# Two-block layer: the second block's feed-forwards with tokens stationary, five of eleven up groups as seven block products for eight

## The chip, the cores and the metric

The kernel runs on one core of one Trainium2 chip. The metric is the device time of one execution in microseconds (us). The figure for the kernel before is the median of 3 runs, 3347.05 us (3345.95 to 3347.32).

## The reference

Two blocks run one after the other over 256 tokens of width 2048, all in fp32. The first block (a state-space branch, a gated delta rule, a gated feed-forward with a short convolution) is not touched. The second block is

```python
h = h + 0.5 * swiglu(rmsnorm_2(h, ffn1_norm[l]), ffn1_w_in[l], ffn1_w_out[l])
u = rmsnorm_2(h, mix_norm[l]) @ w_in_mix[l]
...
h = h + jnp.concatenate([y_pool.astype(h.dtype), y_gla.astype(h.dtype)], axis=-1) @ w_out_mix[l]
h = h + 0.5 * swiglu(rmsnorm_2(h, ffn2_norm[l]), ffn2_w_in[l], ffn2_w_out[l])
```

with a final norm behind it, and

```python
def swiglu(h, w_in, w_out):
    gu = h @ w_in
    gate, up = gu[..., :D_FF], gu[..., D_FF:]
    return (jax.nn.silu(gate) * up) @ w_out
```

`D_FF` is 5632, so that each feed-forward has an up product of 256 x 2048 x 11264 and a down product of 256 x 5632 x 2048. The mix (`w_in_mix`) has four groups of trailing-window means (pool) and four heads of gated linear attention (GLA) with queries, keys, values, an output gate and a gate of low rank.

## The kernel before

**Products in three passes.** Every weight block arrives as 128 x 1024 fp32 (512 KB, `load_w`, line 78, tile `wr`, 4 buffers, on SP's queue). `split_w` (line 113) makes two fp32r tiles of it: ScalarE (ACT) copies the rounded part to `wh` (line 118), VectorE (DVE) subtracts it from the raw block into `wl` (line 119). Each has 3 buffers, and both instructions are raised in priority by 600. Activations are kept as such pairs too. A product is then hi x hi + hi x lo + lo x hi, accumulated in fp32 in a bank of PSUM.

**Four ways to multiply.** `gemm` (line 138) keeps a 128 x 128 weight block stationary and moves 256 tokens, three matmuls a block (lines 127 to 129). `gemm2` (line 153) does the same with two: the hi weights against both token halves of the pair in one matmul of 512 columns (line 162), and the lo weights in one of 256 (line 164). Its result lies in two halves of a bank, which `join` (line 217) adds. `gemm_t` (line 171) keeps 128 tokens stationary and moves 512 weight columns, three matmuls for each 128 tokens and 128 rows of weights (lines 184 to 186). `gemm_halves` (line 194) is a variant for the last quarter. `gemm`, `gemm2` and `gemm_t` use pool `pg` (4 banks); the others' banks come from `bank()` (line 63), pool `px` (4 banks).

**The feed-forward.** `ffn` (line 1024) is called for the first block and twice for the second (`f1`, `f2`; there `conv_w` is None). It cuts the 5632 hidden columns into 44 blocks of 128. `up_group` (line 1030) runs `gemm2` for gate and up of each block, joins, multiplies by the norm's factor spread over partitions, applies Silu and splits the product (`hid`): the hidden tiles come out transposed, as `gemm_t` wants them. `down_group` (line 1055) adds their product into the residual in four quarters of 512 columns by `into_x` (line 1012), which calls `gemm_t`. Group 0 has 4 blocks, groups 1 to 5 have 8; `up_group(c)` runs ahead of `down_group(c - 1)`.

**The mix.** 16 `gemm` for queries, keys and values, 8 for the pool and 8 for the gate, after one narrow product for the low-rank gate. The values are transposed back to tokens on partitions by TensorE in `gla_head` (line 1139, transposes in lines 1182 to 1187).

**What sets the order.** The program is written out in Python and each engine runs its list in order. The tile framework orders the lists by priority (program order, unless raised) and inserts all waits, also for free buffers. Work that is to lie beside products is put in by hand: `flush` (line 134) emits what is in `pend` at a fixed step of a product (`turn`, line 307: TensorE transposes of the residual and the next pairs), and `pump` (line 328) takes one step of the generators in `lanes` (GLA heads, scaling of the residual).

## Time and profile before

| | |
|---|---|
| median of 3 runs | 3347.05 us |
| the profiled execution | 3348.04 us |
| its span (first to last instruction) | 3346.2 us |
| TensorE matmul (PE) busy | 3322.8 us, 99% |
| weight load (PEld) busy | 2873.8 us, 86% |
| DVE busy | 2337.0 us, 70% |
| ACT busy | 1686.4 us, 50% |
| mean DMA rate | 180 GB/s |
| mean granted TensorE clock | 0.999 of 2.4 GHz |

The profiled execution is 1 us above the median, and 1.8 us of it lie outside the span. Matmuls are pipelined and the ends that the profile gives them are modelled: a matmul of 512 columns is listed with some 390 ns, while the next one starts sooner. So the cost of a matmul is read here from start to start, not from the listed duration, and PE's 99% says that it seldom stood still for long, not that it ran at its peak.

### The profile page before, as it was taken

What the parts mean: (1) busy time and instruction counts of PE and PEld (TensorE: products, weight loads), DVE (VectorE), ACT (ScalarE), POOL (GpSimd) and SP (SyncE); (2) the same over time, 40 slices, a digit from 0 to 9 for tenths busy, and PEclk for the clock granted to TensorE, in tenths of its full rate; (3) what the DMA queues carried; (4) which work ended last, traced back from release to release, by engine and by line L of the source; (5) the groups of instructions that cost most, each with busy time, mean ns of one, the idle gap of its engine ahead of it and who ended that gap; (6) DMA issues with size and microseconds to landing.
All of it is one profiled execution on the core that took longest, in us unless ns stands there. A gap on an engine that the chain in (4) does not pass through costs nothing.

```text
span 3346.2 us, 48440 instructions
## 1 busy us (share of the span) xinstructions
PE 3322.8 (99%) x18598; PEld 2873.8 (86%) x18598; DVE 2337.0 (70%) x3718; ACT 1686.4 (50%) x2604; POOL 4.0 (0%) x22
## 2 busy tenths in 40 slices
PE   9999999999999999999999999999999999999998
PEld 8888988888888888888888888889998888888887
DVE  8999987666777767767665656656676666566565
ACT  4566656445554545446444444445464544444444
POOL 0000000000000000000000000000000000000000
PEclk9999999999999999999999999999999999999999
DMA  6555544366666666665666666665546666666665
GB/s 219 155 156 177 176 128 132 111 221 185 185 191 191 187 189 187 188 189 182 189 189 189 187 190 187 187 191 185 151 151 195 185 192 185 189 188 188 189 187 172
DMA packets 169176, 603.42 MB, mean 180 GB/s; under 512 B 18912, under 2 KB 23520, under 8 KB 168432
## 3 DMA queue, kind: packets, MB, share of 16 engines
q1 hardware_dynamic: 168368, 599.29, 58.6%
q8 instruction: 145, 2.38, 0.3%
q10 hardware_dynamic: 576, 1.05, 0.1%
q14 instruction: 87, 0.71, 0.1%
HBM read 598.16 MB, written 2.10 MB: 179 GB/s over the span
## 4 chain that ended last, share of the span: by engine, by line
PE 94%; DVE 5%; issue 1%; ACT 0%; DMA 0%; DVEq 0%; ACTq 0%
PE pt L162 29%; PE pt L164 15%; PE ptt L186 12%; PE ptt L185 12%; PE ptt L184 12%; PE pt L127 3%; PE pt L129 3%; PE pt L128 3%; DVE wl L119 1%; PE pt L228 1%; PE side L857 1%; PE side L868 1%; PE side L603 1%; PE side L638 1%; DVE t L345 0%
## 5 line engine op out<-in xcount | busy, mean ns | idle before, releaser
L119 DVE TENSOR_TENSOR wl<-wr,wh 128x1024 fp32r<-128x1024 f32 x1097 | 1342.4, 1224 | 896.3 <-ACT wh L118 895.0
L118 ACT CAST wh<-wr 128x1024 fp32r<-128x1024 f32 x1097 | 1152.4, 1051 | 1491.0 <-issue 621.6
L162 PE MATMUL pt<-h,wh 128*128 128x512 f32 x4224 | 1487.2, 397 | 0.0
L164 PE MATMUL pt<-h,wl 128*128 128x256 f32 x4224 | 1184.6, 281 | 0.0
L162 PEld LDWEIGHTS pt<-h,wh 128*128 128x128 f32 x4224 | 792.8, 188 | 192.0 <-DVE h L303 0.2
L164 PEld LDWEIGHTS pt<-h,wl 128*128 128x128 f32 x4224 | 798.0, 189 | 1.0
L186 PE MATMUL ptt<-wh,hid 128*128 128x512 f32 x1040 | 408.9, 393 | 0.0
L185 PE MATMUL ptt<-wl,hid 128*128 128x512 f32 x1040 | 407.7, 392 | 0.0
L184 PE MATMUL ptt<-wh,hid 128*128 128x512 f32 x1040 | 405.2, 390 | 0.0
L127 PE MATMUL pt<-h,wl 128*128 128x256 f32 x1024 | 296.1, 289 | 1.0 <-DVE wl L119 1.0
L128 PE MATMUL pt<-h,wh 128*128 128x256 f32 x1024 | 290.4, 284 | 0.0
L129 PE MATMUL pt<-h,wh 128*128 128x256 f32 x1024 | 290.1, 283 | 0.0
L185 PEld LDWEIGHTS ptt<-wl,hid 128*128 128x128 f32 x1040 | 195.3, 188 | 43.6
L184 PEld LDWEIGHTS ptt<-wh,hid 128*128 128x128 f32 x1040 | 195.2, 188 | 43.4
L186 PEld LDWEIGHTS ptt<-wh,hid 128*128 128x128 f32 x1040 | 195.4, 188 | 40.0
L127 PEld LDWEIGHTS pt<-h,wl 128*128 128x128 f32 x1024 | 196.4, 192 | 5.7 <-issue 2.7
L129 PEld LDWEIGHTS pt<-h,wh 128*128 128x128 f32 x1024 | 196.4, 192 | 1.2 <-issue 1.1
L128 PEld LDWEIGHTS pt<-h,wh 128*128 128x128 f32 x1024 | 196.4, 192 | 0.8
L184 PE MATMUL ptt<-wh,h 128*128 128x512 f32 x256 | 103.4, 404 | 0.0
L186 PE MATMUL ptt<-wh,h 128*128 128x512 f32 x256 | 100.2, 392 | 0.0
L185 PE MATMUL ptt<-wl,h 128*128 128x512 f32 x256 | 99.9, 390 | 0.0
L214 ACT ACTIVATE lowh<-pt 128x256 f32<-128x256 f32 x264 | 99.2, 376 | 0.0
(375 smaller groups left out, 3191.2 us busy)
## 6 DMA issues: line engine op xcount, KB each, us to landing
wr<-in_f_up SPq DMA_DIRECT2D x528, 512.0 KB, 3.6
wr<-in_f_down SPq DMA_DIRECT2D x265, 512.0 KB, 3.5
wr<-in_w_qkv SPq DMA_DIRECT2D x48, 512.0 KB, 3.6
wr<-in_w_gs SPq DMA_DIRECT2D x32, 512.0 KB, 3.6
wr<-in_w_gd SPq DMA_DIRECT2D x32, 512.0 KB, 3.6
wr<-in_w_glu SPq DMA_DIRECT2D x32, 512.0 KB, 3.6
wr<-in_w_out SPq DMA_DIRECT2D x32, 512.0 KB, 3.5
wr<-in_w_gla SPq DMA_DIRECT2D x32, 512.0 KB, 3.5
```

What stands on the lines that cost most here:

```text
L118: act.copy(out=hi, in_=raw)
L119: dve.tensor_tensor(out=lo, in0=raw, in1=hi.bitcast(F32), op=ALU.subtract)
L127: pe.matmul(ps, wl, xt[:, 0, :], start=first, stop=False)
L128: pe.matmul(ps, wh, xt[:, 1, :], start=False, stop=False)
L129: pe.matmul(ps, wh, xt[:, 0, :], start=False, stop=last)
L162: pe.matmul(ps.rearrange("p a b -> p (a b)"), hi[:, j, :], xts[k].rearrange("p a b -> p (a b)"), start=k == 0, stop=False, skip_group_chec ...
L164: pe.matmul(ps[:, 0, :], lo[:, j, :], xts[k][:, 0, :], start=False, stop=k == n - 1, skip_group_check=True)
L184: pe.matmul(pss[t], xh, hi[:, j, :], start=k == 0, stop=False)
L185: pe.matmul(pss[t], xh, lo[:, j, :], start=False, stop=False)
L186: pe.matmul(pss[t], xl, hi[:, j, :], start=False, stop=k == n - 1)
L214: act.activation(t, ps[:, 1, :], AF.Copy, scale=scale)
L228: pe.matmul(ps, r3[:, j, :], xs[k], start=k == 0, stop=k == len(xs) - 1)
```

## The change

In the second block's two feed-forwards the up product is turned round: tokens are stationary and 512 weight columns move, as the down product had it. The 5632 hidden columns are eleven groups of 512; groups 0, 1, 2, 6, 8 and 10 are ordinary (`plain`: gate and up by `gemm_t`, 192 matmuls of 512 columns), groups 3, 4, 5, 7 and 9 go through `seven`. That halves the tokens (128 and 128), the 2048 inputs (1024 and 1024) and the columns (gate and up), and forms seven block products where the ordinary way has eight (the Winograd form of Strassen's algorithm): 28 steps of 6 matmuls. For it four sums of the activations are made once (`x_sums`) and four sums of weight blocks in every group; every block or sum that is multiplied is split into its pair. The weight block `b22` is loaded twice. Results come out with tokens on partitions, so that the hidden tiles are transposed by TensorE (`turn_hidden`, 8 transposes a group). `together` takes steps of an ordinary sequence (down products and plain groups, 12 matmuls a step) and of a sequence of sevens in turn; the four `px` banks belong to `seven` meanwhile, and `bank()` gives `pg` banks.

```diff
     def bank():
+        if side_full[0]:
+            return pg.tile([P, 512], F32, tag="pt", name="side2")
         return px.tile([P, 512], F32, tag="side", name="side")
...
+    def gemm_tg(pss, srcs, xts):
...
                 k += 1
                 if k == n // 2:
                     flush()
                 if slices[0]:
                     pump(slices[0] / 4)
-        return pss
+            yield
...
+            def turn_hidden(a, ys):
+                for i in range(2):
+                    pb = v3(bank(), T)
+                    for j in range(2):
+                        for t in range(2):
+                            f = P * (2 * i + j)
+                            pe.transpose(pb[:, j, P * t : P * t + P], a[t][:, f : f + P], ident)
+                    y = ys[i]
+                    act.copy(out=y[:, :, 0, :], in_=pb)
+                    sub(y[:, :, 1, :], pb, y[:, :, 0, :].bitcast(F32))
...
+            def plain(g):
+                a = [hd.tile([P, 512], F32, tag=f"a{t}", bufs=2, name=f"fa{t}") for t in range(2)]
+                pss = []
+                yield from gemm_tg(pss, [A[up][16 * g + i] for i in range(8)], hs)
+                if g == 0:
+                    late[0] = late[0]()
+                rc = late[0]
+                for t in range(2):
+                    act.activation(a[t], pss[t], AF.Silu, scale=rc[:, t : t + 1])
+                pss = []
+                yield from gemm_tg(pss, [A[up][16 * g + 8 + i] for i in range(8)], hs)
+                for t in range(2):
+                    stt(a[t], pss[t], rc[:, t : t + 1], a[t], ALU.mult, ALU.mult)
+                new_ys(g)
+                pend.append(lambda: turn_hidden(a, ys[g]))
+                pump(1)
...
+            def x_sums():
+                for j in range(8):
+                    f = hd.tile([P, 2, T], F32, tag="g", bufs=1, name="xf")
+                    s = hd.tile([P, 4, P], F32, tag="w", bufs=1, name="xs")
+                    for i in range(2):
+                        add(f[:, i, :], hs[j + 8 * i][:, 0, :].bitcast(F32), hs[j + 8 * i][:, 1, :].bitcast(F32))
+                    add(s[:, 0, :], f[:, 0, P:], f[:, 1, P:])
+                    sub(s[:, 1, :], s[:, 0, :], f[:, 0, :P])
+                    sub(s[:, 2, :], f[:, 0, :P], f[:, 0, P:])
+                    sub(s[:, 3, :], f[:, 1, :P], s[:, 1, :])
+                    e = []
+                    for i in range(2):
+                        t = hp.tile([P, 2, 2, P], F32R, tag=f"h{j + 8 * i}", name=f"sx{j}_{i}")
+                        act.copy(out=t[:, 0], in_=s[:, 2 * i : 2 * i + 2, :])
+                        sub(t[:, 1], s[:, 2 * i : 2 * i + 2, :], t[:, 0].bitcast(F32))
...
+            def seven(g):
+                ps = [px.tile([P, 512], F32, tag="side", name="side7") for _ in range(4)]
...
+                for jj in range(4):
+                    b11, b12, b22 = block(jj, 0), block(jj, 1, "ws"), block(4 + jj, 1, "ws")
+                    t1, t3 = (hd.tile([P, 1024], F32, tag="tt", bufs=2, name="tt") for _ in range(2))
+                    t2 = hd.tile([P, 1024], F32, tag=f"t2_{jj}", bufs=1, name="t2")
+                    w1 = split_raw(b11)
+                    with tc.high_priority(offset=600):
+                        sub(t1, b12, b11)
+                        sub(t2, b22, t1)
+                        sub(t3, b22, b12)
+                    passes(ps[0], lambda i: hx(2 * jj + i, 0), w1, **fl)
+                    yield
+                    passes(ps[1], lambda i: sx[2 * jj + i][0], split_raw(t1), **fl)
+                    yield
+                    passes(ps[2], lambda i: sx[2 * jj + i][1], split_raw(t2), **fl)
+                    yield
+                    passes(ps[3], lambda i: sx[2 * jj + i][2], split_raw(t3), **fl)
+                    yield
+                for jj in range(4):
+                    b21, b22 = block(4 + jj, 0), block(4 + jj, 1, "ws")
+                    t4 = hd.tile([P, 1024], F32, tag="tt", bufs=2, name="tt")
+                    with tc.high_priority(offset=600):
+                        sub(t4, b21, t2s[jj])
...
+                act.activation(a[0], ps[0], AF.Silu, scale=rc[:, 0:1])
+                add(a[1], ps[3], gs)
+                add(gs, ps[1], gs)
+                act.activation(a[1], a[1], AF.Silu, scale=rc[:, 1:2])
+                stt(a[0], gs, rc[:, 0:1], a[0], ALU.mult, ALU.mult)
+                stt(a[1], w5, rc[:, 1:2], a[1], ALU.mult, ALU.mult)
+                yield
+                yield
+                new_ys(g)
+                turn_hidden(a, ys[g])
+                yield
...
+                together([first_plain, plain(1), down_g(0), plain(2), down_g(1)], [x_sums(), seven(3), seven(4)])
+                for c in range(2, 5):
+                    together([down_g(c), plain(2 * c + 2)], [seven(2 * c + 1)])
+                if before_last:
+                    before_last()
+                for _ in down_g(5):
+                    pass
+                return
```

The second half of `seven` has three steps for each `jj`, with `b21`, `b22` and `t4`; between the halves three additions of 512 columns bring partial sums together. The first 8 steps of `plain(0)` run alone. `down_g` is `down_group` as a generator, which reads the hidden tiles of two groups.

The norm's factor is now used per token (`rstd_cols`), so that `spread` and its small TensorE product leave the feed-forwards. In the mix, `gemm` gives way to `gemm2` with `join` for queries, keys, pool and gate (24 products), the values come from `gemm_t` (192 matmuls) with tokens on partitions, and the 16 transposes of the values and their copies go. The low-rank product moves behind the first half of the values. The last gain is loaded in four quarters ahead of the last down product and not before the feed-forward. `layout` gives the weights in the new order on the host.

## Rows read from the trace of the kernel before

**Rows 1.** The page: span, and busy time of each engine.

```profile
span 3346.2 us, 48440 instructions
PE 3322.8 (99%) x18598; PEld 2873.8 (86%) x18598; DVE 2337.0 (70%) x3718; ACT 1686.4 (50%) x2604; POOL 4.0 (0%) x22
```

**Rows 2.** The chain that ended last within 1640 to 2260 us, by line.

```profile
by line: PE pt L162 42.8%; PE pt L164 21.7%; PE ptt L186 11.9%; PE ptt L185 11.8%; PE ptt L184 11.7%; PE side L314 0.1%
```

**Rows 3.** Windows: f1, f2, an up pair, a down pair, the mix.

```profile
core 0: us, PE busy (x) PEld busy (x) DVE busy (x) ACT busy (x) POOL busy (x), PEclk, DMA share, GB/s
1542.92:2284.11 741.19, 741.19 (x3908) 633.06 (x3907) 465.87 (x626) 345.26 (x482) 0.00 (x0) 1.00 0.61 187
2598.96:3340.00 741.04, 738.47 (x3883) 630.47 (x3881) 462.07 (x613) 341.70 (x472) 0.00 (x0) 1.00 0.61 186
1699.93:1790.37 90.44, 90.44 (x514) 78.47 (x513) 56.89 (x78) 42.48 (x62) 0.00 (x0) 1.00 0.61 187
1790.37:1834.31 43.94, 43.94 (x194) 36.06 (x193) 24.97 (x27) 17.44 (x18) 0.00 (x0) 1.00 0.63 192
...
2284.10:2508.20 224.10, 223.77 (x1792) 217.70 (x1790) 161.31 (x256) 117.49 (x183) 3.28 (x13) 1.00 0.53 163
```

**Rows 4.** PE's timeline, first and last of 36 steps of `gemm_t`, 25 of `gemm`.

```profile
1794.71 0.39 PE L185 MATMUL ptt<-wl,hid 128*128 128x512 f32 x1
...
1802.95 0.39 PE L185 MATMUL ptt<-wl,hid 128*128 128x512 f32 x1
...
2439.78 0.28 PE L128 MATMUL pt<-h,wh 128*128 128x256 f32 x1
...
2442.78 0.28 PE L129 MATMUL pt<-h,wh 128*128 128x256 f32 x1
```

**Rows 5.** Timeline: eight transposes between two matmuls of `gemm_t`.

```profile
2265.64 0.39 PE L186 MATMUL ptt<-wh,hid 128*128 128x512 f32 x1
...
2265.88 1.04 PE L314 MATMUL side<-ident,xt 128*128 128x128 f32 x8
...
2266.67 0.47 PE L184 MATMUL ptt<-wh,hid 128*128 128x512 f32 x1
...
2266.98 0.39 PE L185 MATMUL ptt<-wl,hid 128*128 128x512 f32 x1
```

**Rows 6.** Groups of instructions by line and shape: count, busy us, mean ns, idle before.

```profile
L119 DVE TENSOR_TENSOR wl<-wr,wh 128x1024 fp32r<-128x1024 f32 x1097 | 1342.4, 1224 | 896.3 <-ACT wh L118 895.0
L118 ACT CAST wh<-wr 128x1024 fp32r<-128x1024 f32 x1097 | 1152.4, 1051 | 1491.0 <-issue 621.6 <-PE ptt L186 549.3 <-PE pt L162 167.7
...
L360 DVE SCALAR_TENSOR_TENSOR xt<-ptt,xt 128x512 f32<-128x512 f32 x96 | 61.6, 683 | 0.8 <-PE ptt L209 0.8
...
L124 DVE TENSOR_TENSOR hid<-fa,hid 128x256 fp32r<-128x256 f32 x132 | 55.3, 419 | 0.0
...
L360 DVE SCALAR_TENSOR_TENSOR wt<-wt,pw,tm 128x128 f32<-128x128 f32 x64 | 20.4, 346 | 2.5 <-ACT tm L610 2.2
...
L864 ACT COPY dsc<-side 128x512 f32<-128x512 f32 x20 | 11.7, 586 | 35.6 <-PE side L863 35.6
```

**Rows 7.** Windows of the first block, where DVE is the busiest.

```profile
80.00:120.00 40.00, 35.38 (x248) 32.66 (x246) 38.61 (x122) 19.61 (x43) 0.00 (x0) 0.98 0.52 162
...
280.00:320.00 40.00, 40.00 (x201) 32.26 (x201) 37.51 (x70) 25.85 (x49) 0.00 (x0) 1.00 0.59 184
```

**Rows 8.** PE's timeline within the second window, 34 steps of `gemm_t`.

```profile
299.72 0.39 PE L185 MATMUL ptt<-wl,h 128*128 128x512 f32 x1
...
307.47 0.39 PE L186 MATMUL ptt<-wh,h 128*128 128x512 f32 x1
```

**Rows 9.** PE's timeline behind the mix: side products among products of `into_x`.

```profile
2508.97 0.40 PE L184 MATMUL ptt<-wh,yp 128*128 128x512 f32 x1
2509.21 1.05 PE L1218 MATMUL side<-sqg,mean_g 128*128 128x256 f32 x4
2509.91 0.58 PE L185 MATMUL ptt<-wl,yp 128*128 128x512 f32 x1
```

**Rows 10.** A wait of PE in the first block, and the clock behind it.

```profile
117.95 0.89 PE L638 MATMUL side<-xa,cmat 128*32 128x256 f32 x2 [3.58 <-DVE xa L345]
...
118.00:124.00 6.00, 6.00 (x31) 4.96 (x32) 4.98 (x13) 2.98 (x8) 0.00 (x0) 0.72 0.56 153
```

**Rows 11.** DMA: loads of up weights to landing; the window with the highest rate.

```profile
wr<-in_f_up SPq DMA_DIRECT2D x528, 512.0 KB, 3.6
...
2280.00:2300.00 20.00, 20.00 (x151) 17.71 (x150) 12.28 (x24) 9.26 (x16) 1.55 (x7) 1.00 0.69 247
```

More of the change, by code (lines that the diff above doesn't have):

```diff
@@ L1 @@
+import itertools
 import math
@@ L1012, in into_x, with into_xg @@
     def into_x(src, n, xts, scale=1.0, fin=None, gain=None, hs=None, halves=False):
+        for _ in into_xg(src, n, xts, scale, fin, gain, hs, halves):
+            pass
+    def into_xg(src, n, xts, scale=1.0, fin=None, gain=None, hs=None, halves=False):
         for q in range(4):
-            g = gemm_halves if halves and q == 3 else gemm_t
-            for t, ps in enumerate(g([src(q, i) for i in range(n)], xts)):
+            pss = []
+            srcs = [src(q, i) for i in range(n)]
+            if halves and q == 3:
+                pss = gemm_halves(srcs, xts)
+            else:
+                yield from gemm_tg(pss, srcs, xts)
+            for t, ps in enumerate(pss):
                 quarter_done(q, t, ps, scale, fin)
@@ new lines, in down_g @@
+            def down_g(c):
+                drain()
+                gs = (2 * c - 1, 2 * c) if c else (0,)
+                tiles = [y[:, j] for g in gs for y in ys[g] for j in range(2)]
+                o = 16 * c - 8 if c else 0
+                n = len(tiles) // 2
+                last = {"fin": fin, "gain": gain, "hs": nxt, "halves": gain is None} if c == 5 else {}
+                yield from into_xg(lambda q, i: A[down][o + n * q + i], n, tiles, scale, **last)
+            sx = []
+            def x_sums():
[13 more added lines that the diff above has]
+                        sub(t[:, 1], s[:, 2 * i : 2 * i + 2, :], t[:, 0].bitcast(F32))
+                        e += [(t[:, 0, c, :], t[:, 1, c, :]) for c in range(2)]
+                    sx.append(e)
+                    yield
@@ L1030, in up_group, with together @@
+            def together(seq, sevens):
+                side_full[0] = True
+                a, b = (itertools.chain(*s) for s in (seq, sevens))
+                for x, y in itertools.zip_longest(a, b):
+                    pass
+                side_full[0] = False
             def up_group(c):
@@ L1059, in down_group @@
                 into_x(lambda q, i: A[down][o + n * q + i], n, tiles, scale, **last)
+            if conv_w is None:
+                first_plain = plain(0)
+                for _ in range(8):
+                    next(first_plain)
+                together([first_plain, plain(1), down_g(0), plain(2), down_g(1)], [x_sums(), seven(3), seven(4)])
[4 more added lines that the diff above has]
+                for _ in down_g(5):
+                    pass
+                return
             prev = up_group(0)
@@ L1086, in late1 @@
         c1 = rstd_cols(n1)
-        b = spread(rstd_cols(n2, pre=c1))
+        c2 = rstd_cols(n2, pre=c1)
         def scale_x():
@@ L1095, in late1 @@
         side.append(scale_x())
-        return b
+        return c2
     h3 = [None] * KT
@@ L1181, in gla_head @@
             act.activation(ktt[:, c, :], pb[:, P * t : P * t + P], AF.Copy, scale=half[:, c % 2 : c % 2 + 1])
-        pv = v3(bank(), T)
-        for t in range(2):
-            for f in range(2):
-                pe.transpose(pv[:, t, P * f : P * f + P], vts[f][:, P * t : P * t + P], ident)
-        vt = scratch(4, [P, 2, T], "vtg")
-        act.copy(out=vt, in_=pv)
         yield
@@ L1198, in gla_head @@
             pk = bank()
-            pe.matmul(pk[:, :T], ktt[:, c, :], vt[:, c // 2, :], start=True, stop=True)
+            pe.matmul(pk[:, :T], ktt[:, c, :], vt[c // 2], start=True, stop=True)
             if c == 0:
@@ L1224, in gla_head @@
         yield
+    gv = []
+    vs = values(0)
+    rm = spread(rc[0])
+    low_rank()
     slices[0] = 1
-    gv = []
     for hd in range(4):
@@ L1231, in tile_kernel @@
         hv = [gp_.tile([P, T], F32, name=f"gv{hd}_{f}") for f in range(2)]
-        for j, t in enumerate((hq, hk, *hv)):
-            ps = gemm(wsrc("w_gla", 4 * hd + j), hs)
-            if j == 0:
-                stt(t, ps, P ** -0.5, rm, ALU.mult, ALU.mult)
-            else:
-                mul(t, ps, rm)
+        if hd == 2:
+            vs = values(1)
+        joined(hq, gemm2(wsrc("w_gla", 2 * hd), hs), P ** -0.5)
+        joined(hk, gemm2(wsrc("w_gla", 2 * hd + 1), hs))
         gv += hv
-        side.append(gla_head(hd, hq, hk, hv))
+        o = 2 * P * (hd % 2)
+        side.append(gla_head(hd, hq, hk, [v[:, o : o + 2 * P] for v in vs], hv))
     def pool_group(g, up):
@@ L1286, in tile_kernel, with load_gb2 @@
     hs = h4
-    gb2 = gains(ctx, 1)
+    gb2 = []
+    def load_gb2():
+        for q in range(4):
+            gb2.append(scratch(q, [P, 512], "gb2"))
+            sp.dma_start(out=gb2[q], in_=A["gain"][1, :, q])
     def fin3(q, t, x):
```

130 lines of the change are left out of this document (96 added, 34 removed).

## The prediction, made before the changed kernel ran

> **What bounds the kernel now.** I read the page's busy times first. TensorE has 99% of the span, DVE 70%, ACT 50% [rows 1]. A busy share is an average over stages, so I went on to the chain of waits inside the first of the two feed-forwards that change: every link but 0.1% is a matmul, of `gemm2` (lines 162, 164) or of `gemm_t` (184 to 186), and no DVE, ACT or DMA stands in it [rows 2]. The windows say the same of both feed-forwards: PE busy 741.19 of 741.19 us and 738.47 of 741.04, DVE 466 and 462, ACT 345 and 342 [rows 3]. So a matmul less is time won here, one for one, for as long as DVE keeps up; and DVE is what the change loads.
>
> **The price of a matmul, start to start.** An up pair of groups (256 blocks of 128 x 128 by `gemm2`) takes 90.44 us [rows 3], 0.3533 us a block. `gemm_t` makes 36 steps in 8.24 us, 0.2289 us a matmul of 512 columns, and `gemm` 25 steps in 3.00 us, 0.1200 us a matmul of 256 [rows 4]. A down pair, 192 matmuls, takes 43.94 us [rows 3], again 0.229 each, with its changes of bank inside.
>
> The Trainium skill, page "TensorE: Matmul & The Clock Gate", section "Wait — 56ns, not 53.3ns?", gives the columns over 2.4 GHz plus 2.5 ns from start to start. By that rule a block of `gemm2` would cost an estimated 0.325 us and a matmul of 512 columns 0.216, turning the product round would win nearly nothing, and the sum below would end at 3322 us. The rows have some 15 ns a matmul on top, and I take the rows.
>
> **Up products.** Removed in each feed-forward: 88 `gemm2` of 16 blocks, 1408 x 0.3533 = 497.4 us. Added: 6 plain groups of 192 matmuls and 5 sevens of 28 x 6 = 168, together 1992 x 0.2289 = 456.0 us. That is 41.4 us each, **-82.8** for both; 28.0 of it comes from turning the product round (2112 x 0.2289 = 483.4 a feed-forward) and 54.9 from the eighth product (5 x 24 matmuls, twice). Taking turns between a plain product and a seven changes the bank oftener; the down pair's price says that this costs nothing.
>
> **Transposes.** Hidden tiles must now be turned, 8 transposes a group. Eight between two matmuls push the second next start from 0.46 to 1.34 us behind [rows 5], 0.88 us. 22 groups: **+19.4**.
>
> **The mix.** Out: 32 `gemm` x 48 x 0.1200 = 184.3 us. In: 24 `gemm2` x 16 x 0.3533 = 135.7 and 192 x 0.2289 = 43.9, together 179.6. 16 transposes of values go, at 0.11 us each 1.8. **-6.5**. The added `join` puts 24 more sums of 256 columns on DVE (0.42 us each [rows 6]), which has 161 of 224 us busy there [rows 3]: nothing. Side steps have fewer products to lie under, and one or two more fall to the end; but side products are fitted in among those of `into_x` there [rows 9]: nothing, or 4 us if not.
>
> The low-rank product, `spread` and the last gain only move; their loads are a few of 0.5 MB or less on SP's queue, and the work beside them covers them. Where `rstd_cols` now makes the first gate wait, the up half has the other two banks and 22 us of matmuls.
>
> Without any new wait this sums to -69.9.
>
> **What could uncover.** DVE first. In the stretch where sevens run, each feed-forward has 640.6 us of PE: 3048 matmuls and 11 turns are 707.4, less 22.0 (the first gate, alone) and 44.8 (the last down, alone). DVE has there 300 splits and 80 weight sums like them at 1.224 us, 465 us; the activation sums, 8 x (4 x 0.419 + 4 x 0.346) = 24.5; and 109 operations of 512 columns at 0.683 for results, additions and hidden tiles, 74.4 [rows 6]. 564 of 640.6, **88%**. In the first half of a seven it is 90%: 11 x 1.224 + 2 x 0.683 = 14.8 of 72 x 0.2289 = 16.5 us. The nearest rows: at 37.5 of 40 us, 94%, PE went 34 steps of `gemm_t` at 0.228 us, undisturbed; at 38.6 of 40, 97%, PE stood still for 4.6 us [rows 7, 8]. 88 to 90% lies on the good side, closer to the first. ACT has 324 casts of 1.051 us in 707, about half.
>
> Locally four waits are possible; each has zero as its lower bound, since there is no work they take away.
>
> - *The three weight sums* of a step stand ahead of the next split on DVE. In the worst order the cast waits for a buffer until the down step's matmuls end; cast, subtraction, three sums and the next subtraction then take 1.05 + 5 x 1.224 = 7.2 us, while PE has 1.37 + 2.75 + 1.37 + 0.23 = 5.7 us of work. 1.5 us late, 40 times: 60 us at most. The sums only need loads that come long before (3.6 us to land [rows 11]) and the framework orders by what is ready, so I take 6.
> - *The activation sums* in 8 steps of 22.0 us together: 24.5 + 8 x 1.224 = 34.3 of DVE, 12.3 over, 24.6 for both at most. Only the last sums are late, and they are wanted some 48 us later; I take 4.
> - *The turn* of a plain group stands right ahead of the down matmuls that read it. ACT copy 0.586 and DVE subtraction 0.683, behind a cast and a subtraction in flight, are 3.55 us at worst against 2.3 us of other work: 1.3 late, 6 times (groups 2, 6 and 8), and 2.7 where nothing lies beside it, twice (group 10): 13 at most. PE's list is filled by what is ready [rows 9]; I take 3.
> - *The end of the fourth group's seven* has no ordinary steps left beside it: two additions, Silu, two products, some 3.8 us, twice, 7.6 at most. The next down can begin with the third group's tiles; I take 1.
>
> **The other queues.** A seven loads 20 blocks for 16, all on SP, whose list waits for free raw buffers. First half: 7 loads of 0.524 MB in 16.5 us, 223 GB/s; 247 was reached [rows 11]. Nothing. The extra `ws` loads stand ahead of plain loads on SP, but wait only for the sums of the step before.
>
> **Sum.** -82.8 + 19.4 - 6.5 + 14 = -55.9 against the profiled execution's 3348.0 us. That lies 1.0 above the median of the runs, so I say **3291**.
>
> **Rivals.**
> 1. *Everything is covered.* The framework fits all waits in, as in the 94% stretch [rows 7, 8]. 3347.05 - 69.9 = 3277. Against it: four places at once. 0.22.
> 2. *DVE becomes the bound: slower.* DVE goes through its list in order and stood 895 us behind ACT's casts before, casts that themselves wait for PE to free a buffer [rows 6]. That was free while DVE had 37% to spare. If the same chain (matmul, buffer, cast, subtraction) keeps it from more than 82% busy in the mixed stretch, this lasts 564 / 0.82 = 688 instead of 640.6 us, 47 more a feed-forward: 3277 + 94 = 3371. It decides from 83.5% downward (564 / 0.835 = 675, 35 us more). For it: cast and subtraction are coupled by three buffers only. Against it: the 94%. 0.10.
> 3. *The clock falls in the waits.* After PE had stood 3.58 us for DVE, the granted clock of the next 6 us was 0.72 [rows 10], so part of it ran at 1.2 instead of 2.4 GHz; 6 x 0.28 = 1.7 us lost on top of the wait. If every unit of a plain group with a seven had one such wait (5 a feed-forward), that is 10 x 5.3 = 53 us: 3330. The Trainium skill, same page, section "A second HAM failure mode: psum-queue depth-cycling", has a kernel whose short pauses at each change of banks let the clock swing; this kernel changes banks far oftener than before. No row of the two feed-forwards shows it: their clock is 1.00 [rows 3]. 0.05.
> 4. *The change does less than it says.* The local waits come to half their bounds together, 53 us of 105: 3277 + 53 = 3330. 0.11.
>
> The forecast itself, 3284 to 3315, has 0.52. The range reaches from rival 1, a little lower for what the mix may give, to over rivals 3 and 4: **3272 to 3342**; rival 2 and the worst of 4 are left out. A measurement of this kernel tells 0.2%, 6.7 us, from no change. Faster: 0.52 + 0.22 + 0.05 and most of 4, less a margin for costs that I don't see, **0.84**; same **0.05**, the upper edge of 4; slower **0.11**.
>
> **What would show it.** In the changed profile: matmuls of 512 columns at 0.229 us also where sevens and plain products take turns; 240 fewer of them in the two feed-forwards than ordinary products would have; each feed-forward some 710 to 717 us long, DVE busy about 599 of it (564, and 24 splits and 8 products outside the mixed stretch), 84%; PE's list of waits with only short entries on `wl`, the transposes and the activation sums; the mix 6 us shorter; clock 1.00. Wrong would be: DVE above 94% busy for long, or below 84% with PE waiting for `wl`; a feed-forward above 735 us; a chain of waits in which DVE has more than a tenth.

## The result and the profile after

The changed kernel takes **3308.7 us** (median of 4 runs, 3307.0 to 3309.9), the kernel before 3347.2 in the same comparison: ratio 0.9883, 95% interval 0.9866 to 0.9900, 38.5 us less. Forecast were 3291, that is 56 us less. The sign and the range held; the gain is two thirds of the one forecast. The profiled execution took 3307.0 us.

The page of the changed kernel: span, busy times and the chain that ended last by engine; behind them two rows of its DMA list (KB each, median us from issue to landing) [rows 1, 11]. The last row is the chain by engine in the kernel before.

```profile
span 3305.2 us, 44334 instructions
PE 3263.8 (99%) x16530; PEld 2742.3 (83%) x16530; DVE 2568.6 (78%) x3748; ACT 1777.3 (54%) x2523; POOL 4.0 (0%) x22
PE 84%; DVE 10%; DMA 3%; issue 2%; ACT 1%; DVEq 0%; SPq 0%; ACTq 0%
...
wr<-in_f_up SPq DMA_DIRECT2D x448, 512.0 KB, 3.8
ws<-in_f_up SPq DMA_DIRECT2D x120, 512.0 KB, 4.5
...
PE 94%; DVE 5%; issue 1%; ACT 0%; DMA 0%; DVEq 0%; ACTq 0%
```

PE is still listed as 99% busy, but DVE's share of the chain over the whole kernel has risen from 5 to 10%, and that of loads from 0 to 3%. In the first feed-forward (f1) before, no DVE and no DMA stood in the chain [rows 2]; in the changed kernel DVE's splits and weight sums have 13% of it there and loads of `wr` 7% (1560 to 2220 us).

The same three stretches in the changed kernel, by windows: first feed-forward, mix, second feed-forward with the kernel's end.

```profile
core 0: us, PE busy (x) PEld busy (x) DVE busy (x) ACT busy (x) POOL busy (x), PEclk, DMA share, GB/s
1542.70:2265.40 722.70, 713.96 (x3167) 583.20 (x3167) 579.40 (x631) 388.48 (x430) 0.00 (x0) 1.00 0.62 207
2265.40:2572.35 306.95, 306.90 (x1612) 259.25 (x1611) 222.27 (x345) 167.90 (x269) 3.27 (x13) 1.00 0.52 175
2572.35:3305.20 732.85, 714.17 (x3147) 582.36 (x3145) 577.80 (x621) 385.39 (x421) 0.00 (x0) 0.99 0.61 204
```

Windows cut in the same way before have 741.20, 315.06 and 747.24 us. So f1 gives 18.5 us, the mix 8.1 and f2 14.4, together 41.0, the whole difference of the spans. In f1 PE was busy in every microsecond before [rows 3]; now it stands still for 8.7 of 722.7, and more in f2. This understates it, since a matmul behind a pause is listed longer. Counted from start to start (what lies beyond 0.2288 us for a matmul of 512 columns, beyond 0.11 for a transpose, each by more than 0.05), the losses are 17.3 us in f1 and 19.9 in f2, against less than 2 us in either before: **37 us**, where 14 were forecast. The question of the experiments is where they come from.

PE's list of waits in the changed kernel, from 1540 us to the end (us in total, times, longest):

```profile
PE side L1131 <- DVE wl L126: 9.3, 11, 1.8
PE ptt L202 <- DVE hid L367: 3.3, 4, 1.2
PE side L1130 <- ACT wh L125: 2.3, 2, 1.1
PE ptt L201 <- DVE wl L126: 1.7, 4, 0.6
PE side L1061 <- DVE fa L376: 0.9, 2, 0.6
PE ptt L200 <- ACT wh L125: 0.5, 2, 0.3
```

The largest is a seven's matmul (lines 1130 to 1132) that waits for the low part of its weights, DVE's subtraction of line 126. Two fifths of all losses sit in one place in each feed-forward: the end of group 4's seven, whose last steps have no ordinary block beside them. The windows there:

```profile
1816.00:1820.00 4.00, 4.00 (x19) 3.31 (x18) 4.00 (x6) 2.34 (x3) 0.00 (x0) 1.00 0.35 127
1820.00:1824.00 4.00, 3.24 (x14) 2.10 (x13) 3.89 (x4) 3.38 (x4) 0.00 (x0) 1.00 0.62 190
1824.00:1828.00 4.00, 1.58 (x6) 0.74 (x4) 4.00 (x4) 1.04 (x1) 0.00 (x0) 1.00 0.80 245
1828.00:1832.00 4.00, 3.51 (x12) 2.50 (x13) 2.99 (x6) 1.81 (x3) 0.00 (x0) 0.57 0.94 333
```

and what DVE and PE do in them, by the timeline (start us, us, instruction, what ended the idle time before):

```profile
1821.04 2.55 DVE L126 TENSOR_TENSOR wl<-wr,wh 128x1024 fp32r<-128x1024 f32 x2
1823.52 1.22 DVE L367 TENSOR_TENSOR t<-ws,tt 128x1024 f32<-128x1024 f32 x1
1824.65 1.22 DVE L367 TENSOR_TENSOR tt<-ws 128x1024 f32<-128x1024 f32 x1
1825.79 1.22 DVE L126 TENSOR_TENSOR wl<-wr,wh 128x1024 fp32r<-128x1024 f32 x1
1826.92 1.22 DVE L126 TENSOR_TENSOR wl<-tt,wh 128x1024 fp32r<-128x1024 f32 x1
...
1826.21 0.50 PE L1130 MATMUL side<-wh,sx 128*128 128x512 f32 x1 [1.13 <-ACT wh L125]
1828.19 0.80 PE L1131 MATMUL side<-wl,sx 128*128 128x512 f32 x1 [1.48 <-DVE wl L126]
1828.78 0.63 PE L1132 MATMUL side<-wh,sx 128*128 128x512 f32 x1
1829.21 0.63 PE L1130 MATMUL side<-wh,sx 128*128 128x512 f32 x1
...
1828.06 0.68 DVE L364 TENSOR_TENSOR fa<-side,gs 128x512 f32<-128x512 f32 x1
1830.99 1.26 PE L1061 MATMUL side<-ident,fa 128*128 128x128 f32 x7 [0.30 <-DVE fa L376]
```

Group 4's last product ends at 1822.4 us. What ought to follow on DVE are its results, then PE turns them and the next down step begins. Instead the framework has put the start of the next seven (group 5) there: on DVE its splits and two of its three weight sums (`t` and `tt`, 1823.52 to 1825.79), on PE its first two products, the second of which is the one that waits in the rows above. DVE is busy for 11.9 of 12 us (1816 to 1828), group 4's results come behind all this, from 1828.06, the turn at 1831.0, and the next ordinary block at 1832.1. Behind the waits the granted clock is 0.57 on average over the window, and matmuls start 0.43 us apart instead of 0.229, as at the lower of its two levels, 1.2 GHz. By the count from start to start this place loses 6.3 us in f1 and 9.3 in f2.

Elsewhere DVE itself stands still; its two largest waits from 1560 to 2220 us:

```profile
DVE wl L126 <- ACT wh L125: 87.0, 85, 1.7
DVE tt L367 <- DMA wr<-in_f_up: 24.6, 22, 2.5
```

The second is new: a weight sum at the head of DVE's list, whose block (`b11` or `b21`, a `wr` tile) has not landed.

### The profile page after: what moved, and what is told of

It reads as the page before. It is cut to its first block, busy times and chain, and to the rows that moved or that the text cites. A ratio compares the mean times of both kernels' runs of the same rounds, so it can differ in the third digit from the quotient of the medians.

```text
span 3305.2 us, 44334 instructions
## 1 busy us (share of the span) xinstructions
PE 3263.8 (99%) x16530; PEld 2742.3 (83%) x16530; DVE 2568.6 (78%) x3748; ACT 1777.3 (54%) x2523; POOL 4.0 (0%) x22
## 4 chain that ended last, share of the span: by engine, by line
PE 84%; DVE 10%; DMA 3%; issue 2%; ACT 1%; DVEq 0%; SPq 0%; ACTq 0%
PE ptt L202 15%; PE ptt L201 15%; PE ptt L200 15%; PE pt L169 13%; PE pt L171 6%; DVE wl L126 4%; PE side L1131 3%; PE side L1132 3%; PE side L1130 3%; DMA wr<-in_f_up 3%; PE pt L134 1%; PE pt L136 1%; PE pt L135 1%; PE pt L244 1%; DVE tt L367 1%
## 5 line engine op out<-in xcount | busy, mean ns | idle before, releaser
L169 PE MATMUL pt<-h,wh 128*128 128x512 f32 x1792 | 633.0, 398 | 0.0
L171 PE MATMUL pt<-h,wl 128*128 128x256 f32 x1792 | 502.6, 281 | 0.0
L200 PE MATMUL ptt<-wh,h 128*128 128x512 f32 x1088 | 427.6, 393 | 0.0
L201 PE MATMUL ptt<-wl,h 128*128 128x512 f32 x1088 | 423.9, 390 | 0.6 <-DVE wl L126 0.6
L202 PE MATMUL ptt<-wh,h 128*128 128x512 f32 x1088 | 424.1, 390 | 0.0
L169 PEld LDWEIGHTS pt<-h,wh 128*128 128x128 f32 x1792 | 336.4, 188 | 81.8 <-issue 1.0
L171 PEld LDWEIGHTS pt<-h,wl 128*128 128x128 f32 x1792 | 338.3, 189 | 0.6
L200 PEld LDWEIGHTS ptt<-wh,h 128*128 128x128 f32 x1088 | 204.3, 188 | 43.5 <-ACT wh L125 1.2
L201 PEld LDWEIGHTS ptt<-wl,h 128*128 128x128 f32 x1088 | 204.3, 188 | 43.4 <-DVE wl L126 1.7
L202 PEld LDWEIGHTS ptt<-wh,h 128*128 128x128 f32 x1088 | 204.3, 188 | 43.1 <-issue 0.4
L126 DVE TENSOR_TENSOR wl<-tt,wh 128x1024 fp32r<-128x1024 f32 x120 | 146.7, 1223 | 78.0 <-ACT wh L125 77.5
L134 PE MATMUL pt<-h,wl 128*128 128x256 f32 x512 | 149.3, 292 | 0.4 <-DVE wl L126 0.4
L136 PE MATMUL pt<-h,wh 128*128 128x256 f32 x512 | 145.4, 284 | 0.0
```

Source lines behind the costliest of these rows:

```text
L126: dve.tensor_tensor(out=lo, in0=raw, in1=hi.bitcast(F32), op=ALU.subtract)
L134: pe.matmul(ps, wl, xt[:, 0, :], start=first, stop=False)
L136: pe.matmul(ps, wh, xt[:, 0, :], start=False, stop=last)
L169: pe.matmul(ps.rearrange("p a b -> p (a b)"), hi[:, j, :], xts[k].rearrange("p a b -> p (a b)"), start=k == 0, stop=False, skip_group_chec ...
L171: pe.matmul(ps[:, 0, :], lo[:, j, :], xts[k][:, 0, :], start=False, stop=k == n - 1, skip_group_check=True)
L200: pe.matmul(pss[t], xh, hi[:, j, :], start=k == 0, stop=False)
```

## The experiments

All times are medians; the kernel before was run beside each set (3347.3 to 3348.1 us), and ratios are to it. Differences are against the changed kernel's 3308.7 (0.9866 to 0.9900) unless said otherwise. Edits are to the changed kernel.

### What turning the product round is worth without the sevens

```diff
-    together([first_plain, plain(1), down_g(0), plain(2), down_g(1)], [x_sums(), seven(3), seven(4)])
...
+    for step in (plain(0), plain(1), down_g(0), plain(2), plain(3), down_g(1), ..., plain(9), down_g(4), plain(10)):
+        for _ in step:
+            pass
```

> All eleven up groups plain, none as seven products; the rest of the change stays. It parts the change into what the turned product and the mix bring and what the eighth product brings. If the terms of the sum are right and only sevens bring new waits: turning -28.0, transposes +19.4, mix -8.0 from 3347.2, that is 3331, each feed-forward some 737 us, and PE hardly ever behind DVE. Then sevens have brought 3331 - 3308.7 = 22 us net of 54.9. If instead turning the product round brings waits of its own (the rival): 3340 or more.

Measured: 3326.3 us (3325.6 to 3326.9), ratio 0.9933 (0.9919 to 0.9948). Windows of f1 and f2, and the only wait in PE's list there:

```profile
1542.40:2275.55 733.15, 732.88 (x3284) 606.09 (x3283) 392.06 (x401) 317.52 (x349) 0.00 (x0) 1.00 0.57 189
2582.63:3323.80 741.17, 732.07 (x3267) 604.63 (x3265) 391.00 (x397) 315.28 (x341) 0.00 (x0) 1.00 0.57 189
PE ptt L200 <- ACT wh L125: 0.5, 2, 0.3
```

Turning and mix bring 21.8 us, 5 to 7 more than had been worked out from the rows of before, and PE hardly waits. f1's 3168 matmuls take (733.15 - 120 x 0.11) / 3168 = 0.2273 us each, not 0.2289. The sevens then bring 3326.3 - 3308.7 = 17.6 us net of the 54.9 that their missing products are worth: **37 us are given back, all of it in the sevens' stretch**.

### The activation sums ahead, so that no steps are left alone

```diff
+    early = x_sums()
     for _ in range(8):
         next(first_plain)
+        next(early)
-    together([first_plain, ...], [x_sums(), seven(3), seven(4)])
+    together([first_plain, ...], [seven(3), seven(4)])
```

> The eight steps of activation sums are taken beside the first eight steps of the first plain group, so that the two sequences of the first mixed stretch are 64 and 62 steps long and no step of a seven stands alone. Theory 'end of the stretch' (six of 70 steps alone, where DVE needs more than PE; 6.2 and 8.7 us lost there): 3308.7 - 15 = 3294, and no loss above 2 us at that place. Rival 'DVE is the bound as a whole': the loss moves elsewhere, 3303 or more.

Measured: 3322.2 us (3317.7 to 3324.1), ratio 0.9923 (0.9907 to 0.9940): slower, a miss. Its two feed-forwards say why. In f2, where nothing else happened, the loss from start to start fell from 19.9 to 13.3 us, and the one at group 4's end is gone. In f1 it grew from 17.3 to 33.1. PE's waits from 1560 to 1640 us, and ACT's timeline:

```profile
PE ptt L200 <- ACT fa L1080: 6.8, 1, 6.8
PE ptt L201 <- DVE wl L126: 2.5, 2, 1.9
...
1611.71 0.71 ACT L1116 CAST sx<-xs 128x256 fp32r<-128x256 f32 x2
1612.43 1.28 ACT L1080 ACT_TABLE_LOAD   x1
1616.81 1.26 ACT L1080 ACTIVATE fa<-ptt,rc 128x512 f32<-128x512 f32 x2 [3.09 <-DVE rc L361]
```

Only f1 has `late1`, whose norm factors (`rc`) DVE works out, and which then scales the residual, while group 0 runs. With the activation sums in the same list, `rc` came at 1616.8, and group 0's Silu held its banks until then. The end of group 4 can be mended, but not at that price.

### The weight sums without their priority

```diff
-    with tc.high_priority(offset=600):
-        sub(t1, b12, b11)
...
+    sub(t1, b12, b11)
...
```

> The weight sums are no longer raised by 600 in priority, the splits still are. Theory 'DVE stands at the head of its list for loads of sums' (25 and 26 us of DVE behind DMA): these waits shrink, the splits come earlier, 3308.7 - 5 to - 13, that is 3296 to 3304. Rival 'sums must be early since the splits of sums need them': the splits come later, 3312 or more. If DVE's total load is what counts, 3307 to 3310.

Measured: 3305.8 us (3302.5 to 3307.6), ratio 0.9871 (0.9856 to 0.9886). The interval overlaps that of the changed kernel: the priority neither costs nor brings what can be told. DVE's standing for loads stays, 25.6 us in f1.

### The weight sums on GpSimd

```diff
+            def wsub(o, a, b):
+                pool_e.tensor_tensor(out=o, in0=a, in1=b, op=ALU.subtract)
...
-        sub(t1, b12, b11)
+        wsub(t1, b12, b11)
...
```

> The weight sums (80 a feed-forward) go from DVE to GpSimd, which stands idle. DVE loses 98 us a feed-forward and all waits for loads of sums. Theory 'DVE's load': the waits of PE for wl nearly vanish except at the end of the first stretch, 3285 to 3295, if one sum takes GpSimd no more than some 5 us (there are 16 in a seven of about 120 us). Rival 'GpSimd is slow or slows DVE' (DVE's subtraction of 1.22 us gets longer, or splits wait for sums): slower than 3308.7.

Measured: 3388.8 us (3378.2 to 3392.7), ratio 1.0115 (1.0096 to 1.0134). Two rows of its groups by form:

```profile
L126 DVE TENSOR_TENSOR wl<-wr,wh 128x1024 fp32r<-128x1024 f32 x1017 | 1409.3, 1389 | 469.2 <-ACT wh L125 452.8
L1104 POOL TENSOR_TENSOR tt<-ws,wr 128x1024 f32<-128x1024 f32 x40 | 116.2, 2905 | 2192.9 <-DMA wr<-in_f_up 1926.4
```

A sum takes GpSimd 2.9 us in the row shown and 2.8 to 3.2 by its operands. DVE's subtraction grew from 1.22 to 1.39 us on average over the whole kernel (1.54 from f1 on, where the sums are), so that more came back than the 195 us that DVE was to be rid of (DVE busy 2619 us against 2569). The Trainium skill, page "SBUF — State Buffer", section "Who interferes with whom", says that a DVE instruction with two SBUF inputs contends with a GpSimd instruction that reads SBUF; these two rows agree.

### One list of steps

```diff
-    together([first_plain, plain(1), down_g(0), plain(2), down_g(1)], [x_sums(), seven(3), seven(4)])
-    for c in range(2, 5):
-        together([down_g(c), plain(2 * c + 2)], [seven(2 * c + 1)])
+    together([first_plain, plain(1), down_g(0), plain(2), down_g(1), plain(6), down_g(2),
+              plain(8), down_g(3), plain(10), down_g(4)],
+             [x_sums(), seven(3), seven(4), seven(5), seven(7), seven(9)])
```

> The mixed stretch is written as one list of steps with no stop between its parts: plain group 6 stands before the down step of groups 3 and 4, plain 8 and 10 likewise before theirs, so that the six steps that were left alone at the end of group 4 have ordinary blocks beside them, and only three steps (without block products) stand alone at the very end. If those six steps, each with 1.37 us of matmuls against 1.22 us of VectorE, are the place where about 15 us of the 36 us of waits arise (6.3 in the first feed-forward, 9.4 in the second), the time falls from 3308.7 to about 3294, and the excess between matmuls near 1820:1832 and 2850:2870 is gone. If VectorE is short over the whole stretch and the loss only moves to the steps after, the time stays above 3303.

Measured: 3307.3 us (3300.2 to 3309.9), ratio 0.9877 (0.9862 to 0.9891): no difference, and the profiled run is the fastest of the four. The window of group 4's end, and PE's waits at the new end, 2195 to 2225 us:

```profile
1816.00:1836.00 20.00, 20.00 (x90) 16.55 (x89) 14.65 (x15) 11.68 (x12) 0.00 (x0) 1.00 0.65 210
PE side L1061 <- DVE fa L376: 4.7, 1, 4.7
```

The old loss is gone entirely, and a new one of 6.6 us in each feed-forward has come at the end of group 9, whose results are now worked out, turned and read with nothing beside them. So the place is where it was said to be, but the time is not won: a seven's end without cover has moved. (Of the six steps that the expectation counts only three are products; the others are the results and the turn.)

The same list without the priority:

> The same list of steps, and the weight sums without their priority (they stand in the order in which they are written). The order alone gave 3305.83 against 3308.7. If the two losses are apart, about 3291; if the priority only matters where nothing stands beside the seven's steps, the same as the one list of steps alone, within 3 us.

Measured: 3311.5 us (3311.0 to 3312.5), ratio 0.9893 (0.9878 to 0.9908). With two losses apart it should have been the faster one. The gain of 3 us above was no gain.

### No weight sums at all

This kernel leaves the sums out and so does not compute the layer.

```diff
-    raw = hd.tile([P, 1024], F32, tag=tag, bufs=2, name="ws")
+    raw = hd.tile([P, 1024], F32, tag=tag, bufs=4, name="ws")
...
-    t1, t3 = (hd.tile([P, 1024], F32, tag="tt", bufs=2, name="tt") for _ in range(2))
...
+    t1, t2, t3 = b12, b22, b22
...
+    t4 = b21
```

> Leaves out the sums of weight blocks: the seven products take the blocks as they are loaded, so matmuls, loads and splits keep their number, and 16 subtractions of 1.22 us per seven (195 us of VectorE in all) are gone; the raw blocks get four buffers in place of two. If the waits come from the sums (VectorE's time, and its standing still for the sums' loads), nearly all of the 36 us go: about 3275 to 3280. If they come from the activation sums, the turning and the start of each group, the time stays above 3295.

Measured: 3282.3 us (3279.9 to 3284.2), ratio 0.9803 (0.9787 to 0.9819), **26.4 us less**. From start to start it loses 7.8 + 7.3 us, of which 5.4 and 4.2 are at group 4's end. Windows before, at and behind that end in f1 (1580:1816, 1816:1840, 1840:2200):

```profile
1580.00:1816.00 236.00, 236.00 (x1055) 195.06 (x1054) 164.49 (x170) 127.34 (x133) 0.00 (x0) 1.00 0.67 214
1816.00:1840.00 24.00, 21.29 (x87) 16.52 (x86) 15.86 (x16) 12.74 (x14) 0.00 (x0) 0.93 0.51 170
1840.00:2200.00 360.00, 360.00 (x1600) 297.12 (x1599) 241.84 (x227) 192.66 (x195) 0.00 (x0) 1.00 0.65 211
```

Everywhere but there PE is busy without a gap in f1 (0.8 us are missing in f2). So the weight sums make the losses, all but some 10 us at group 4's end and a few elsewhere. What this does not tell is whether it is their work (195 us) or the standing that they bring; the raw blocks also had four buffers here in place of two.

### The loads of the sums on another queue

```diff
-    sp.dma_start(out=raw, in_=src)
+    pool_e.dma_start(out=raw, in_=src)
```

> The six of fourteen... that is, the 12 blocks of each seven that only feed sums or are kept raw are loaded by GpSimd's queue in place of SyncE's, where they stand behind loads that wait for their own buffers; nothing else changes. VectorE stands still 24.6 us in the first mixed stretch and 26.3 us in the second for such loads. If that is what makes splits late, the time falls by about 10 us, to 3298, and VectorE's waits for the loads shrink. If VectorE's waits only fill time that it would idle anyway, the time stays within 3 us of 3308.7. If a GpSimd queue lands later or slows VectorE, it is over 3312.

Measured: 3315.8 us (3312.3 to 3318.7), ratio 0.9905 (0.9890 to 0.9920). DVE's standing is not less:

```profile
DVE tt L367 <- DMA wr<-in_f_up: 28.3, 21, 3.0
```

The row names the block: `wr`, not `ws`. What is late is the one block that the seven also splits, which comes through the ring of four `wr` buffers; SP stands there for a buffer that a split must free (SP's waits for `wl`: 445 us in that stretch of the changed kernel). The edit moved the loads that were in time. Why it is 7 us slower than the changed kernel stays open.

### The same sums from blocks that are there

```diff
-    sub(t1, b12, b11)
+    sub(t1, b12, b22)
...
-    sub(t4, b21, t2s[jj])
+    sub(t4, t2s[jj], t2s[jj])
```

> Every weight sum is still made, of the same size and at the same place, but the first and the last of each set no longer read the block that the seven has just asked for: they read blocks that are there already (so the products get other numbers than the algorithm's). VectorE's work is the same (16 sums of 1.22 us per seven); only its standing for the loads of those two blocks, 24.6 us in the first mixed stretch and 26.3 in the second, is taken away. Leaving the sums out altogether gave 3282.3, that is 26.4 us less than with them. If those 26 us came from VectorE standing still at the head of its list, the time falls to 3285 to 3292. If they came from VectorE's 195 us of work itself, it stays within 4 us of 3308.7.

Measured: 3310.2 us (3308.0 to 3315.2), ratio 0.9894 (0.9877 to 0.9910): no gain, which by the expectation would speak for DVE's work. The windows say otherwise. The same three in f1, and DVE's wait for loads from 1560 to 2220 us:

```profile
1580.00:1816.00 236.00, 235.41 (x1049) 193.67 (x1048) 196.72 (x209) 127.14 (x135) 0.00 (x0) 1.00 0.63 210
1816.00:1840.00 24.00, 14.86 (x55) 10.89 (x54) 19.21 (x20) 9.71 (x11) 0.00 (x0) 0.79 0.53 175
1840.00:2200.00 360.00, 359.46 (x1593) 295.65 (x1592) 283.18 (x266) 190.89 (x192) 0.00 (x0) 1.00 0.63 209
...
DVE tt L367 <- DMA ws<-in_f_up: 12.3, 12, 1.9
```

The edit took away only half of the standing (24.6 us in the changed kernel): the sums now wait at times for the other two blocks of their set.

The time in which PE is not busy, us, by such windows (in f2 2600:2842, 2842:2880 and 2880:3230):

| kernel | outside group 4's end, f1 + f2 | at group 4's end, f1 + f2 |
|---|---|---|
| changed kernel | 4.8 + 5.0 | 3.7 + 4.7 |
| no weight sums | 0.0 + 0.8 | 2.7 + 2.0 |
| one list of steps (group 9's end lies behind these windows) | 3.7 + 4.1 | 0 + 0 |
| sums from blocks that are there | 1.1 + 1.6 | 9.1 + 10.4 |
| own buffer (below) | 3.8 + 5.9 | 7.4 + 7.3 |
| one list, own buffer (below) | 8.6 + 6.5 | 0 + 0 |
| the same, sums spread (below) | 6.9 + 4.6 | 0 + 0 |

Where ordinary steps lie beside the sevens, most of PE's waits went with half of the standing, with all of DVE's work left in place. Counted from start to start, the losses in those windows are 19.3 us in the changed kernel, 8.2 here and 3.5 with no weight sums: some 11 of the 16 us that the sums cost there. At group 4's end the edit does the opposite (28.0 us lost against 15.7): sums that are ready earlier are also taken earlier, three of the next set stand ahead of group 4's results, and PE waits up to 2.6 us for a split there, and 4.6 us in f1 and 5.9 us in f2 for the results. So there are two mechanisms, and in this run one paid for the other. This rests on one execution of each kernel.

### An own buffer for the block that is late

```diff
-    if tag is None:
-        return load_w(src)
-    raw = hd.tile([P, 1024], F32, tag=tag, bufs=2, name="ws")
+    raw = hd.tile([P, 1024], F32, tag=tag or "wb", bufs=2 if tag else 1, name=tag or "wb")
...
-    w5 = hd.tile([P, 512], F32, tag="w", bufs=1, name="w5")
+    w5 = ps[2]
```

> The block that a seven splits and sums (one per four or three steps) gets a raw buffer of its own, so it no longer stands in the ring of four behind ordinary blocks; the space comes from keeping one of the group's sums in the PSUM bank that is done (one of VectorE's operations reads other operands, none is added). If VectorE's standing for this block is what made the splits late, its waits for loads in the first mixed stretch fall from 24.6 us to under 8, and the time falls by 10 to 20 us, to 3289 to 3299. If the standing only fills time that VectorE would idle anyway, or the block still comes late because SyncE's list is in order, the time stays within 4 us of 3308.7.

Measured: 3312.6 us (3308.2 to 3317.6), ratio 0.9896 (0.9881 to 0.9911). The largest waits for loads in f1 fell from 24.6 and 3.0 us only to

```profile
DVE tt L367 <- DMA wb<-in_f_up: 16.5, 19, 2.3
DVE wl L126 <- DMA wb<-in_f_up: 4.5, 3, 1.5
```

With the smaller ones it is 23.5 us in all, against 28.3. The trace shows why the load hardly starts earlier: there is one own buffer, and 78 of the 79 later loads into it are issued within 0.06 us of the end of the split that frees it. So the load waits for its own buffer now, in place of one of the ring, and this way of mending it fails; two own buffers were not tried.

### One list, own buffer, and cover for the last seven's end

Beside the two edits above, the last down step starts with group 10's blocks, and its first two steps stand beside the end of group 9:

```diff
-    gs = (2 * c - 1, 2 * c) if c else (0,)
+    gs = (10, 9) if c == 5 else (2 * c - 1, 2 * c) if c else (0,)
...
+    first = n // 2 if c == 5 else 0
-    yield from into_xg(lambda q, i: A[down][o + n * q + i], n, tiles, scale, **last)
+    yield from into_xg(lambda q, i: A[down][o + n * q + (i + first) % n], n, tiles, scale, **last)
```

> The own buffer, with the one list of steps (no stop after group 4), and with the last down step beginning with group 10's blocks, so that two ordinary steps stand beside the end of group 9. The one list alone gave 3307.3; in its trace the loss near 1820 was gone, and a new one of 6.6 us per feed-forward stood at the end of group 9 (the turning waits 4.7 us for VectorE's evictions). If the three losses are apart, the end gives 8 to 12 us, and the buffer what it gives by itself: 3280 to 3290. If VectorE is simply short over the whole stretch, about 3300.

Measured: **3295.4 us** (3290.8 to 3298.2), ratio 0.9843 (0.9828 to 0.9858), 13 us less than the changed kernel and 12 less than the one list. Both ends now have cover; what is left in PE's list is the wait for splits:

```profile
PE ptt L201 <- DVE wl L126: 14.3, 17, 1.3
PE side L1061 <- DVE fa L376: 1.1, 3, 0.4
```

That is 5 us above the upper end of what was expected. Group 9's end gave what it should: from start to start, behind 2200 and 3230 us, 3.4 us are lost in place of 13.5 with the one list. The buffer gave nothing: in the windows of the table PE stands still for 15.1 us, against 7.8 with the one list alone, so that the buffer may even cost something.

### The same with the sums spread over the steps

```diff
-    with tc.high_priority(offset=600):
-        sub(t1, b12, b11)
-        sub(t2, b22, t1)
-        sub(t3, b22, b12)
...
+    with tc.high_priority(offset=600):
+        sub(t1, b12, b11)
     passes(ps[1], lambda i: sx[2 * jj + i][0], split_raw(t1), **fl)
...
```

> The kernel with the one list of steps and the own buffer (3295.4, its matmuls waiting 14.3 us for VectorE's splits in 17 places), with each weight sum made directly ahead of its own split, one per step, in place of three at the head of each set of four steps; number, size and operands of all work are the same. Three sums in a row take VectorE 3.4 us, and the splits ready ahead cover one step of each kind, 4.1 us. If the remaining waits come from such bursts, most of the 14.3 us go: 3282 to 3289. If they come from VectorE's work as such, or from the load of a seven's block being late, the time stays within 4 us of 3295.4. If a sum so close to its split is itself late (sum, cast and subtraction in a row take 3.5 us), it is over 3300.

Measured: **3290.2 us** (3286.3 to 3293.5), ratio 0.9828 (0.9814 to 0.9841). PE's largest wait:

```profile
PE ptt L201 <- DVE wl L126: 11.1, 15, 1.2
```

It fell by 3 us of 14, not by most of it, and the two intervals overlap, so that the three sums in a row are a small part at best. DVE's standing for the own block is still 26.7 us in f1 (28.6 without the spreading). Against the changed kernel the interval lies apart: this version is 18.5 us faster, and the fastest that computes the layer.

## Why the prediction was right and wrong

**What held.** PE bounded the kernel, and each matmul less was time won as long as DVE kept up. **The eighth product** and **turning** gave what was priced, and some 5 us more; matmuls of 512 columns start 0.2273 us apart in long runs, less than the 0.2289 of the prediction. The Trainium skill's rule for that step, page "TensorE: Matmul & The Clock Gate", section "Wait — 56ns, not 53.3ns?", would be 0.216 for 512 columns (an estimate from its formula): the measured value lies nearer to the row. (The prediction put the rows some 15 ns above that rule; by its own numbers it is 11 to 14.) **The mix** gave 8.1 for 6.5. **The turn** of a plain group, taken as 3, cost nothing where no seven ran: the kernel without sevens has 0.5 us of waits in both feed-forwards. Beside sevens `hid` was late for 3.3 us [PE's list above], and not at all without weight sums.

**Rival 2, DVE as the bound, did not come**, though its mechanism did on a small scale. DVE is busy 579 of 723 us, 80%, not 599 of some 714: sums and splits one behind the other start 1.14 us apart (1823.52, 1824.65, 1825.79), where the prediction counted the listed 1.224. Of the signs of being wrong that were named, DVE below 84% with PE waiting for `wl` came. DVE with more than a tenth of the chain came in f1's mixed stretch (13%); over the whole kernel it is 10%, of which 5 were there before. **Rival 3**, the clock, came only behind the waits at group 4's end (0.57 in f1, 0.50 in f2) and cost some 2 us in f1 and 3 in f2; in the other windows of both feed-forwards it is 1.00, although plain and seven steps change banks all the time. What the same page of the Trainium skill, section "A second HAM failure mode: psum-queue depth-cycling", tells of another kernel, a clock that swings with short pauses at each change of banks, is not seen here. **Rival 4** had the right kind: 37 us of waits lie between the 14 of the forecast and its 53. That the total still fell within the forecast's own 3284 to 3315 is in part luck: 23 us more of waits than forecast stand against some 7 us more from turning and the mix.

**The step that failed is the 14 us of local waits**, and in it two terms, priced too low; a third, priced too high, is below.

- *The weight sums, taken as 6 with a bound of 60.* Leaving them out gives 26.4 us, some 6 of them at group 4's end. "The sums only need loads that come long before" is the sentence that was wrong. 3.6 us to land [rows 11] was read as short, but what counts is when the load may start: a `wr` buffer comes free only with a split, four blocks earlier, so whenever DVE has caught up with its list, the block of the next set is still under way, and DVE stands at the head of its list for it, 24.6 us in f1. The loads also landed later than in rows 11: 4.2 us (median) from 1560 to 2220 us, and 3.0 to 5.8 us for the ten that stand in the chain there, so that a late start and a slow landing are not parted. With half of the standing gone, PE's idle time outside group 4's end fell from 9.8 to 2.7 us. Three sums in a row, the mechanism that the prediction had in mind, explains at most a few us (measured with the one list of steps).
- *The end of the fourth group's seven, taken as 1 with a bound of 7.6.* It cost 6.3 + 9.3 us, twice the bound. The prediction counted the results behind the last product (two additions, Silu, two products) as if they came at once, left out that three steps of matmuls stand alone too, and held that "The next down can begin with the third group's tiles". In PE's list neither held: the next down's blocks stand behind the turn, and ahead of it stand two products of the next seven, for whose splits and sums DVE lets the results wait. About 10 us of it stay with no sums at all; with ordinary blocks beside it, all of it goes.

The *activation sums*, taken as 4, cost next to nothing. The last of them ends at 1604 us in f1 and 2609 in f2. Some 5 us are lost from start to start between 1600 and 1640 and between 2630 and 2670 us, but behind DVE's standing for blocks of weights; without weight sums 0.1 us is lost there, with the activation sums in place. Pulling them ahead of group 0's factors in f1 cost 16 us there, so their place was well chosen.

What stays open: whether a load of `b11` and `b21` started early enough (a deeper ring of raw blocks, or two own buffers) would bring the rest; it was not tried. That standing is the main cause outside group 4's end rests on one run, which took half of it away and whose total did not move: it is read from its windows, not from its time. The 5 us that are left there above the kernel without sums may be the other half or DVE's work.

## What to carry to other kernels

When work is added to an engine that runs its list in order, its busy share says little: with DVE at 80%, 37 of the 55 us that the sevens save were given back. Ask of each added instruction when its operands can be there at the earliest (which buffer must come free first, and who frees it), and what stands behind it in the list. When two kinds of steps are dealt out in turns, count both to the end: the kind that is left over runs without the cover that its price assumed, and the framework fills the hole with work of the next stage, ahead of what the next stage waits for.

## What the hardware showed beyond that

GpSimd's subtraction of 128 x 1024 fp32 took 2.8 to 3.2 us against DVE's 1.22, and DVE's own rose to 1.54 on average from f1 on in that run (1.52 for those that split a sum in `tt`). Loads of 512 KB issued from GpSimd's queue landed in 4.3 us like those of SyncE (4.5), at 0.53 us of GpSimd each. Behind 3.4 us of waits of PE between 1822 and 1829 us the granted clock was 0.57 from 1828 to 1832, in part at the lower level of 1.2 GHz, and matmuls of 512 columns started 0.43 us apart; from 1832 to 1836 it was 1.00. In f2 it was 0.50 from 2864 to 2868 and 0.84 from 2868 to 2872.
